# A transformer block's token mixing on one core: another order of projections and convolution taps, and shared softmax steps

## The chip, the core and the metric

The kernel runs on one core of a Trainium2 chip. A core has a matrix engine (TensorE; PE in the profile, with its weight loads as PEld), three engines for everything else (VectorE, DVE; ScalarE, ACT; GpSimd, POOL) and a queue for data transfers (SyncE, SP). Each engine takes its instructions strictly in the order in which the program lists them and waits at an instruction until its inputs are ready and its output's place is free. [...]

The metric is device time in microseconds (us) of one execution. The time before is 1881.29 us, the median of three runs.

## The reference

One layer on 512 tokens of width 2048, all in 32-bit floats. Three mixers share one input projection and one output projection, and a feed-forward part follows:

```python
h = _rms_norm(x, norm1_g[l])
proj = h @ w_in[l]
aq, ak, av, bu, bg, cq, ck, cv = jnp.split(proj, splits, axis=-1)
aq = _rms_norm(aq.reshape(B, S, A_HEADS, HEAD_DIM), a_q_g[l])   # ak, cq, ck likewise
out_a = _dilated_mixture(aq, ak, av).reshape(B, S, A_WIDTH)     # 8 heads x 64
out_b = _conformer_conv(bu, bg, conv_w[l], conv_b[l], conv_ln_g[l], conv_ln_b[l])
out_c, _ = _band_attention(cq, ck, cv, C_WINDOW - 1, sinks=c_sinks[l])
x = x + jnp.concatenate([out_a, out_b, out_c], axis=-1) @ w_out[l]
h2 = _rms_norm(x, norm2_g[l])
x = x + (jax.nn.silu(h2 @ w_gate[l]) * (h2 @ w_up[l])) @ w_down[l]
```

- **A**: 8 heads; three causal patterns of keys (the last 128, every 4th, every 16th), combined by their softmax denominators.
- **B**: 512 channels; `u * sigmoid(gate)`, a causal convolution of each channel over 31 tokens, a layer norm over channels, `silu`.
- **C**: 16 query heads on 2 key heads, the last 128 keys, and a learned sink for each head: the row maximum is `max(scores, sink)` and `exp(sink - maximum)` joins the denominator.

## The kernel before

Tokens lie along the free axis and channels along the 128 partitions, so a tile is 128 channels by 512 tokens. Each 32-bit operand is split into a high and a low part, and a product is three matmuls (`mm3`, lines 311 to 314): high by high, high by low, low by high.

**Stages.** The norm and the first four projection tiles (the A values) come first. Then 26 projection tiles follow one after the other in the order of `PROJ`; a name is mixer, kind and number, so `cq3` holds the queries of C heads 3 and 11, and `bu0` and `bg0` the input and gate of the first convolution tile. While TensorE projects, the other engines work on tiles already projected: the head norms, the two attentions, and the convolution, whose 124 taps (4 tiles of 31) are one VectorE instruction each (`tap`, line 507). Then comes the output projection, in two halves of 8 rows each in the order of `ROWS`, and the feed-forward part, where the change touches nothing.

**Ticks.** The order is written by hand with a clock of ticks (`Ticks`). A step is put down for a number of ticks from now; the program calls `tick()` between matmuls, and what is due then is listed behind the matmuls already listed. A tick is no time but a place in the order of every engine. A projection has 8 ticks with 6 matmuls between two of them, so the 26 projections hold ticks 0 to 207. The first two output tiles share 8 ticks of 6 matmuls (`first_two`); after that a tick stands behind every 12 matmuls, except in the first tile of the second half, where each of its 8 rows (3 matmuls) has one.

**What is due when.**

- `head_scales` (line 561): after a query or key tile is projected, the transpose comes `SQ` = 3 ticks later, then the square, the sum (`total`) and the power -1/2 on GpSimd (`power`, line 586), one tick each.
- `do_k` (line 613) goes on from there: 2 ticks later `widen` copies the scales to a full tile (line 623), then a transpose (`flip`, line 630), `scale`, the copies of each head's 64 rows to the other half (`twin`, two transfers), and after `TD` = 2 ticks the high and low parts (lines 648, 653). `box["k at"]` is the tick before which no head may start on this key.
- `attention` (A) and `grouped_attention` (C) take the first tick that the keys, the queries and the head before allow (`head_at`), and put down each head from there: `scores`, `top` (the maximum and minus its scaled value), `exps` (with the row sums), `norm` (the division), the transposes of the probabilities (`flip`), their high and low parts, the product with the values (`weigh`), and the two halves of its sum. An A head takes 7 ticks, a C head 6; C heads come in pairs that share a key head, one tile of probabilities each.
- `Head` (line 728) holds the small statistics of one head. For C a unit `u` is two of the four 128-token tiles, so `top`, `exps` and `norm` run twice for each head: on VectorE lines 784 and 786 (minus the maximum, with the sink), 803 and 808 (the denominator and its reciprocal), on ScalarE line 798 (the sink's exponential), on GpSimd line 811 (the division).
- `split_mix` (line 986) makes the high and low part of a row of the output projection; the low part of a C row is GpSimd's (line 991), of the others VectorE's. Where a row is not in place when its matmuls come, `split_rows` makes it there.
- The taps start at tick `TAPS_FROM` = 19 and follow every 1.6 ticks, with a pause of 9 ticks from tick 205; the layer norm (`ln_sum` to `ln_out`) follows at fixed distances.

Weights come through SP in the order in which they are used; each is split by ScalarE (line 289) and VectorE (line 290) two units ahead of its use.

Of the kernel before, what the change touches and what calls it, by code (L numbers as in the profile page):

```python
# [9 lines left out]
F32 = mybir.dt.float32  # L10
# [22 lines left out]
TAP_TICKS = 1.6  # L33
TAPS_FROM = 19
# [5 lines left out]
SQ, VD, TD, EV = 3, 4, 2, 1  # L40
# [82 lines left out]
def kernel(ctx: ExitStack, tc: tile.TileContext, xT, wi, wo, wgu, wd, cst_in, outT):  # L123
# [604 lines left out]
    class Head:  # L728


        def __init__(self, kind, box, name, h, number):
# [3 lines left out]
            d = cp.tile([P, 4, NT], F32, name=f"{self.name}d", tag="soft", bufs=6)  # L735
            self.mx, self.nm, self.den, self.rd = (d[:, i] for i in range(4))
            self.banks, self.es = {}, {}

        def start(self, t0):
            _, _, step, s1, sx, s2, *_ = C_TICKS if self.grouped else A_TICKS  # L740
            for u in range(len(self.us)):
# [3 lines left out]
                ticks.after(tu + s1 + sx, self.exps, u)  # L745
                ticks.after(tu + s1 + sx + s2, self.norm, u)
# [16 lines left out]
        def top(self, u):  # L763
# [13 lines left out]
            for i, k0, n, o in reversed(self.us[u]):  # L777
                if self.grouped and i:
# [4 lines left out]
                                               accum_out=mx[:, i:i + 1])  # L783
            nc.vector.scalar_tensor_tensor(nm[:, s], mx[:, s], -1.0, rq[:, s, h], op0=ALU.mult, op1=ALU.mult)
            if self.grouped:
                nc.vector.tensor_scalar(nm[:, s], nm[:, s], nsink[:, self.number:self.number + 1], None, op0=ALU.min)

        def exps(self, u):
# [8 lines left out]
            if self.grouped:  # L797
                nc.scalar.activation(self.mx[:, s], self.nm[:, s], AF.Exp, bias=col(C_SINK + self.number))

        def norm(self, u):  # L800
            e, den, rd, s = self.es[u], self.den, self.rd, self.tiles(u)
            if self.grouped:
                nc.vector.tensor_add(den[:, s], den[:, s], self.mx[:, s])
            else:
                for i, k0, n, o in self.us[u]:
                    nc.vector.scalar_tensor_tensor(e[:, o:o + n], e[:, o:o + n], 1.0, mult_a[:, T - n:],
                                                   op0=ALU.mult, op1=ALU.mult, accum_out=den[:, i:i + 1])
            nc.vector.reciprocal(rd[:, s], den[:, s])
            if self.grouped:
                own = e[:, 2 * u * P:2 * (u + 1) * P].rearrange("p (i k) -> p i k", k=P)  # L810
                nc.gpsimd.tensor_mul(own, own, rd[:, s, None].to_broadcast([P, 2, P]))
                return
# [86 lines left out]
    def grouped_attention(two):  # L899
# [6 lines left out]
        def heads(h):  # L906
# [68 lines left out]
            for t in range(2):  # L975
                ticks.after(t0 + at_flip + t, flip, t)
# [689 lines left out]
```

## Time and profile before

| | |
|---|---|
| median of three runs (1879.92 to 1881.71) | 1881.29 us |
| the profiled execution | 1881.01 us |
| its span, first to last instruction | 1879.0 us |
| TensorE busy | 1868.2 us, 9784 matmuls |
| VectorE busy | 1458.2 us, 2347 instructions |
| ScalarE busy | 1333.2 us, 1886 instructions |
| GpSimd busy | 1219.5 us, 812 instructions |
| mean granted TensorE clock | 0.998 of full |

In a row, `out<-in` names tiles as the program does, and L and a number is a line of the kernel. "a <- b" in a list of waits means that a's engine stood idle until b was done. A matmul's duration in a row is longer than the distance from one to the next, since they overlap. The granted clock is the share of full speed that the chip's throttle gave TensorE. Idle time of an engine matters only if a chain from it reaches the last instruction.

### The profile page before, as it was taken

The numbers are of one execution on the slowest core, as the hardware profiler recorded it, in microseconds if no ns is written. First come the engines' busy times: TensorE is split into PE (matmuls) and PEld (weight loads), VectorE is DVE, ScalarE is ACT, GpSimd is POOL, SyncE is SP. The second block draws the span as 40 slices with busy tenths as digits, with TensorE's granted clock in tenths as the row PEclk, the third lists the DMA queues.
The fourth block names the chain that finished last, engine by engine and source line by source line (L and its number), as shares of the span: only waits on it lengthen the run. The fifth ranks groups of instructions, "written<-read, shape, count | busy, mean of one in ns | idle before, by whom it ended". The sixth has DMA issues, their size and how long they took to land.

```text
span 1879.0 us, 28424 instructions
## 1 busy us (share of the span) xinstructions
PE 1868.2 (99%) x9784; PEld 1605.4 (85%) x9784; DVE 1458.2 (78%) x2347; ACT 1333.2 (71%) x1886; POOL 1219.5 (65%) x812
## 2 busy tenths in 40 slices
PE   9999999999999999999999999999999999999999
PEld 7888878888888888888888888888888888888888
DVE  7578988997679777777777777777777677778887
ACT  6345545553556888888878888788887887777675
POOL 5014433462155878787877878788787867766786
PEclk9999999999999999999999999999999999999999
DMA  7333332434342354443544435344455475578984
GB/s 271 122 110 108 93 96 85 126 100 145 107 146 88 120 175 145 157 168 130 182 138 163 163 133 183 134 164 161 142 178 192 152 239 184 197 251 285 308 243 124
DMA packets 157984, 301.07 MB, mean 160 GB/s; under 512 B 29968, under 2 KB 69008, under 8 KB 157840
## 3 DMA queue, kind: packets, MB, share of 16 engines
q1 hardware_dynamic: 157696, 299.25, 48.4%
q8 instruction: 77, 1.26, 0.3%
q14 instruction: 67, 0.55, 0.1%
q10 hardware_dynamic: 144, 0.01, 0.0%
HBM read 241.27 MB, written 50.33 MB: 155 GB/s over the span
## 4 chain that ended last, share of the span: by engine, by line
PE 92%; DVE 5%; ACT 1%; issue 1%; POOL 1%; DMA 0%; DVEq 0%; POOLq 0%; ACTq 0%
PE out L1255 51%; PE out L1397 16%; PE o L313 3%; PE o L314 3%; PE o L312 3%; DVE wl L290 1%; PE cq L312 1%; PE cq L314 1%; PE cq L313 1%; DVE y L514 1%; PE in L313 1%; PE in L312 1%; PE in L314 1%; PE ak L314 1%; PE ak L312 1%
## 5 line engine op out<-in xcount | busy, mean ns | idle before, releaser
L1255 PE MATMUL out<-h,wh 128*128 128x512 f32 x2464 | 588.4, 391 | 0.0
L1255 PEld LDWEIGHTS out<-h,wh 128*128 128x128 f32 x2464 | 452.7, 188 | 87.5
L1255 PEld LDWEIGHTS out<-h,wl 128*128 128x128 f32 x2464 | 316.1, 191 | 12.5 <-DVE wl L295 0.4
L1255 PE MATMUL out<-h,wl 128*128 128x256 f32 x2464 | 320.3, 283 | 0.2 <-DVE wl L295 0.2
L1397 PE MATMUL out<-wh,a 128*128 128x512 f32 x896 | 221.2, 389 | 0.0
L1397 PEld LDWEIGHTS out<-wh,a 128*128 128x128 f32 x896 | 168.2, 188 | 34.9
L289 ACT CAST wh<-w 128x1024 fp32r<-128x1024 f32 (+1 forms) x93 | 96.8, 1042 | 129.3 <-PE o L313 43.2
L290 DVE TENSOR_TENSOR wl<-w,wh 128x1024 fp32r<-128x1024 f32 (+1 forms) x93 | 117.1, 1261 | 44.9 <-ACT wh L289 44.5
L1397 PE MATMUL out<-wl,a 128*128 128x512 f32 x448 | 119.7, 389 | 0.0
L1397 PEld LDWEIGHTS out<-wl,a 128*128 128x128 f32 x448 | 84.1, 188 | 17.4
L514 DVE SCALAR_TENSOR_TENSOR y<-bu,cst,y 128x511 f32<-128x511 f32 (+14 forms) x120 | 94.4, 787 | 0.7
L1255 PE MATMUL out<-a,wh 128*128 128x512 f32 x330 | 80.1, 391 | 0.0
L1255 PEld LDWEIGHTS out<-a,wh 128*128 128x128 f32 x330 | 60.3, 188 | 11.4
L312 PE MATMUL o<-mh_c,wh 128*128 128x512 f32 x128 | 51.2, 400 | 0.0
L313 PE MATMUL o<-ml_c,wh 128*128 128x512 f32 x128 | 50.1, 392 | 0.5 <-POOL ml_c L991 0.5
L314 PE MATMUL o<-mh_c,wl 128*128 128x512 f32 x128 | 50.1, 391 | 0.0
L1442 DVE TENSOR_TENSOR Y<-Y,out 128x512 f32<-128x512 f32 x48 | 30.7, 682 | 19.4 <-PE out L1397 19.3
L1255 PEld LDWEIGHTS out<-a,wl 128*128 128x128 f32 x330 | 43.3, 191 | 2.2
L1255 PE MATMUL out<-a,wl 128*128 128x256 f32 x330 | 44.1, 283 | 0.0
L312 PE MATMUL cq<-hh,wh 128*128 128x512 f32 x96 | 39.3, 410 | 0.0
L430 POOL TENSOR_TENSOR ssum<-ssum,sq 128x512 f32<-128x512 f32 x15 | 26.8, 1785 | 19.1 <-ACT sq L429 18.6
L314 PE MATMUL cq<-hh,wl 128*128 128x512 f32 x96 | 38.3, 399 | 0.0
(3395 smaller groups left out, 5170.7 us busy)
## 6 DMA issues: line engine op xcount, KB each, us to landing
od<-a SPq DMA_DIRECT2D x140, 256.0 KB, 4.7
a<-od SPq DMA_DIRECT2D x140, 256.0 KB, 6.4
w<-in_wi SPq DMA_DIRECT2D x59, 512.0 KB, 3.6
w<-in_wo SPq DMA_DIRECT2D x32, 512.0 KB, 3.5
x<-in_xT SPq DMA_DIRECT2D x16, 256.0 KB, 7.4
xr<-in_xT SPq DMA_DIRECT2D x16, 256.0 KB, 3.7
x2d<-xr SPq DMA_DIRECT2D x16, 256.0 KB, 2.0
yd<-z SPq DMA_DIRECT2D x16, 256.0 KB, 5.3
```

Source lines behind the costliest of these rows:

```text
L289: nc.scalar.copy(hi[:, :n], t[:, :n])
L290: eng.tensor_sub(lo[:, :n], t[:, :n], hi[:, :n].bitcast(F32))
L312: nc.tensor.matmul(out, wh, xh, start=start, stop=False)
L313: nc.tensor.matmul(out, wh, xl, start=False, stop=False)
L314: nc.tensor.matmul(out, wl, xh, start=False, stop=stop)
L430: eng.tensor_add(acc, acc, sq)
L514: nc.vector.scalar_tensor_tensor(yconv[j][:, i:], hconv[j][:, :T - i], c, yconv[j][:, i:], op0=ALU.mult, op1=ALU.add)
L1255: nc.tensor.matmul(out, lhs[:, s], rhs, start=begin, stop=last and low == flip[0] and x is xs[-1], skip_group_check=True)
L1397: nc.tensor.matmul(to[h], x[:, h * P:(h + 1) * P], v[:, j], start=sub == 0 and h not in started, stop=sub == 1 and n in (len(todo) - 1, le ...
L1442: nc.vector.tensor_add(t, t, b)
```

## The change

- **Order of projections.** `bu1` and `bg1` come right behind `bu0` and `bg0`, before any C tile; `bu2` and `bg2` come two tiles earlier. The host lays the weight columns out in the new order.
- **Taps.** The first 47 steps from tap to tap are one tick each, the later ones 1.8 ticks, and the last two tiles' taps are 6 ticks later on top. The layer norm follows the last tap by two ticks.
- **Keys.** `KW` = 4 ticks instead of 2 between the power and `widen`; `k at` grows by `KW`.
- **C heads.** The statistics of the two heads of a pair share one tile. Minus the maximum and the sink are taken once for each head, for all four token tiles, after the second unit's maximum, and the sink's exponential once with the second unit; the first unit's exponentials come one tick later. The denominator and its reciprocal are taken once for both heads together, and GpSimd divides each head's whole tile in one instruction; all of it stands at the tick where the second head's second unit was divided before.
- **Rows.** Another order of the C rows in the output projection (`w_out` is laid out to match), and three of them instead of two are split during the last projection, at ticks 1, 3 and 5 of it.

```diff
-TAP_TICKS = 1.6
-TAPS_FROM = 19
+TAPS_FROM, TAPS_FAST, TAP_TICKS = 19, 47, 1.8
+TAPS_2 = 6
...
-SQ, VD, TD, EV = 3, 4, 2, 1
+SQ, KW, VD, TD, EV = 3, 4, 4, 2, 1
...
-PROJ = ("av0 av1 av2 av3 bu0 bg0 cv ck cq0 cq3 bu1 bg1 cq1 cq5 cq2 "
-        "cq7 bu2 bg2 ak2 cq4 cq6 bu3 bg3 ak0 aq0 ak1 aq1 aq2 ak3 aq3").split()
-ROWS = "c0 c1 c2 c4 c5 c3 c7 c6 a0 a1 b2 b1 b0 b3 a2 a3".split()
+PROJ = ("av0 av1 av2 av3 bu0 bg0 bu1 bg1 cv ck cq0 cq3 cq1 cq5 bu2 "
+        "bg2 cq2 cq7 ak2 cq4 cq6 bu3 bg3 ak0 aq0 ak1 aq1 aq2 ak3 aq3").split()
+ROWS = "c0 c3 c1 c5 c2 c7 c4 c6 a0 a1 b2 b1 b0 b3 a2 a3".split()
...
-            ticks.after(2, widen, r)
+            ticks.after(KW, widen, r)
-        box["k at"] = ticks.now + SQ + TD + 10
+        box["k at"] = ticks.now + SQ + KW + TD + 10
@@ Head.start @@
-                ticks.after(tu + s1 + sx, self.exps, u)
-                ticks.after(tu + s1 + sx + s2, self.norm, u)
+                if not self.grouped:
+                    ticks.after(tu + s1 + sx, self.exps, u)
+                    ticks.after(tu + s1 + sx + s2, self.norm, u)
+                else:
+                    ticks.after(t0 + step + s1 + 1 + u, self.exps, u)
@@ Head.top @@
+            if self.grouped and u == 0:
+                return
+            if self.grouped:
+                s = slice(0, NT)
             nc.vector.scalar_tensor_tensor(nm[:, s], mx[:, s], -1.0, rq[:, s, h], op0=ALU.mult, op1=ALU.mult)
             if self.grouped:
-                nc.vector.tensor_scalar(nm[:, s], nm[:, s], nsink[:, self.number:self.number + 1], None, op0=ALU.min)
+                nc.vector.tensor_scalar(nm, nm, nsink[:, self.number:self.number + 1], None, op0=ALU.min)
@@ Head.exps @@
-            if self.grouped:
-                nc.scalar.activation(self.mx[:, s], self.nm[:, s], AF.Exp, bias=col(C_SINK + self.number))
+            if self.grouped and u == 1:
+                nc.scalar.activation(self.mx, self.nm, AF.Exp, bias=col(C_SINK + self.number))
@@ Head.norm @@
-                nc.vector.tensor_add(den[:, s], den[:, s], self.mx[:, s])
...
-                own = e[:, 2 * u * P:2 * (u + 1) * P].rearrange("p (i k) -> p i k", k=P)
-                nc.gpsimd.tensor_mul(own, own, rd[:, s, None].to_broadcast([P, 2, P]))
@@ grouped_attention, heads @@
+            d = cp.tile([P, 4, 2, NT], F32, name=f"{name}d2", tag="softs", bufs=2)
+            for k, one in enumerate(pair):
+                one.stats(d[:, :, k])
+            def norm():
+                _, top, den, rd = (d[:, i].rearrange("p k i -> p (k i)") for i in range(4))
+                nc.vector.tensor_add(den, den, d[:, 0].rearrange("p k i -> p (k i)"))
+                nc.vector.reciprocal(rd, den)
+                for k, one in enumerate(pair):
+                    own = one.es[0].rearrange("p (i k) -> p i k", k=P)
+                    nc.gpsimd.tensor_mul(own, own, one.rd[:, :, None].to_broadcast([P, NT, P]))
...
+            ticks.after(t0 + step + s1 + sx + s2, norm)
...
-        at_tap = TAPS_FROM + int(n * TAP_TICKS)
-        ticks.after(at_tap + TAP_PAUSE * (at_tap >= PAUSE_FROM), tap, j, i)
-    t_ln = TAPS_FROM + 1 + int(len(taps) * TAP_TICKS) + TAP_PAUSE
+        at_tap = TAPS_FROM + min(n, TAPS_FAST) + int(max(n - TAPS_FAST, 0) * TAP_TICKS) + TAPS_2 * (j >= 2)
+        at_tap += TAP_PAUSE * (at_tap >= PAUSE_FROM)
+        ticks.after(at_tap, tap, j, i)
+    t_ln = at_tap + 2
...
-            for n, row in enumerate(ROWS[:2]):
-                ticks.after(4 + n, split_mix, row)
+            for n, row in enumerate(ROWS[:3]):
+                ticks.after(1 + 2 * n, split_mix, row)
```

More of the change, by code (lines that the diff above doesn't have):

```diff
@@ L734, in __init__, with stats @@
             self.number = number
-            d = cp.tile([P, 4, NT], F32, name=f"{self.name}d", tag="soft", bufs=6)
+            self.banks, self.es = {}, {}
+        def stats(self, d):
             self.mx, self.nm, self.den, self.rd = (d[:, i] for i in range(4))
-            self.banks, self.es = {}, {}
         def start(self, t0):
@@ L838, in head @@
             one = Head("a", box, mi, h, None)
+            one.stats(cp.tile([P, 4, NT], F32, name=f"{mi}{h}d", tag="soft", bufs=2))
             ph, pl = {}, {}
```

10 lines of the change are left out of this document (3 added, 7 removed).

## The prediction

> **What bounds the kernel now.** I read the page's busy shares first, then the list of who waited for whom on TensorE (columns: waiter, releaser, total us, times, longest).
>
> ```profile
> PE 1868.2 (99%) x9784; PEld 1605.4 (85%) x9784; DVE 1458.2 (78%) x2347; ACT 1333.2 (71%) x1886; POOL 1219.5 (65%) x812
> ```
>
> ```profile
> PE ak2t L630 <- ACT ak2wide L623: 3.8, 1, 3.8
> PE idle L410 <- DVE bones L343: 1.4, 1, 1.4
> PE ak1t L630 <- ACT ak1wide L623: 0.8, 1, 0.8
> PE a10s L758 <- DVE ak1l L653: 0.8, 1, 0.8
> PE o L313 <- POOL ml_c L991: 0.5, 2, 0.3
> PE out L1255 <- DVE wl L295: 0.2, 1, 0.2
> ```
>
> TensorE is busy 99% of the span and idle 7.5 us in all. The change adds and removes no matmul, so it can return only these waits, and what they drag behind them. Work taken from VectorE, ScalarE or GpSimd is worth nothing by itself: it counts only where it shortens one of these six lines, or makes a seventh. The longest has a second price, which stands in windows of 2 us (length, busy time of each engine, granted clock, DMA):
>
> ```profile
> 256.00:258.00 2.00, 0.00 (x0) 0.00 (x0) 2.00 (x4) 0.46 (x1) 1.50 (x1) 0.65 0.00 0
> 258.00:260.00 2.00, 1.79 (x7) 1.60 (x8) 0.44 (x3) 1.74 (x7) 0.61 (x1) 0.50 0.73 209
> 260.00:262.00 2.00, 2.00 (x6) 1.62 (x5) 1.94 (x4) 0.00 (x0) 0.00 (x0) 0.50 0.48 127
> 262.00:264.00 2.00, 2.00 (x7) 1.52 (x7) 0.91 (x3) 0.16 (x1) 0.61 (x1) 0.65 0.85 181
> ...
> 354.00:357.00 3.00, 2.21 (x12) 1.60 (x11) 2.94 (x6) 1.37 (x3) 2.27 (x2) 1.00 0.19 22
> ```
>
> After 3.8 us without work TensorE restarts at half clock. Lost work is busy time times the missing share: 1.79 x 0.50 + 2.00 x 0.50 + 2.00 x 0.35 = 2.6 us. So this one wait costs 3.8 + 2.6 = 6.4 us. The last row holds one of the waits of 0.8 us: its clock stays 1.00, so I price those at 0.8 each. The Trainium skill (TensorE: Matmul & The Clock Gate, section Terms) prices throttled time at time x (1 - K/N); the rows hold (0.35 + 0.50 + 0.50 + 0.35) x 2.0 / 0.50 = 6.8 us at half clock, so an estimate by that page is 3.4, and 0.8 more would come back. The trace bears it out only in part, since the clock had fallen 1.6 us before TensorE had work again.
>
> **The change, part by part.** All ticks below are the planner's arithmetic: a projection is 8 ticks of six matmuls, so the projection with place n in the order after the first four ends before tick 8n.
>
> *The key chain (KW).* The chain behind the 3.8 us, in order of time:
>
> ```profile
> 253.30 0.39 PE L314 MATMUL cq<-h,wl 128*128 128x512 f32 x1
> 253.98 0.39 PE L314 MATMUL cq<-h,wl 128*128 128x512 f32 x1
> 254.21 1.69 POOL L933 TENSOR_TENSOR c20bl<-c20pl,mask_c 128x512 fp32r<-128x512 f32 x1 [1.36 <-DVE c20pl L927]
> 255.87 1.63 POOL L586 TENSOR_TENSOR ak2r<-ak2v,nhalf 128x8 f32<-128x8 f32 x1
> 257.54 0.62 ACT L623 COPY ak2wide<-ak2r 128x512 f32<-128x512 f32 x1 [3.49 <-POOL ak2r L586]
> 258.21 1.12 PE L630 MATMUL ak2t<-ident,ak2wide 128*128 128x128 f32 x4 [3.84 <-ACT ak2wide L623]
> ```
>
> The power on GpSimd stands behind a mask product of an earlier head pair; ScalarE and TensorE, in order, block one after the other. ak2 ends at tick 120 in both orders. The transpose moves from tick 129 to 131: two ticks, twelve matmuls of 0.227 us (the first two rows are three matmuls apart, 0.68 us), 2.7 us. Also, in the new order the pair before it starts at ticks 103 and 109 instead of 105 and 111 (pairs now run from 67 without a gap, every 12 ticks), so its mask products are due by tick 124, two ticks ahead of the power at 126, not level with it. Without the 1.69 us product in front the widened row would stand at 258.2 - 1.7 = 256.5; TensorE asked for it at 258.21 - 3.84 = 254.4 and now asks 2.7 later, at 257.1. **Gain 6.4**; at the worst end, with the product still in front, 258.2 - 257.1 = 1.1 us remains, too short for the clock if the 0.8 us row is any guide (gain 5.3). The ak1 transpose gets the same 2.7 us against 0.8: gain 0.8. The a1 heads wait for "k at", which grows by 4 while the key's low part is due only 2 ticks later, so the 0.8 for ak1l goes too: gain 0.8. In all **8.0**. What the wait queues is ScalarE's exponentials; they now run before the widening. The two copies of a key between partition halves are issued two ticks later on SP, behind a weight load at worst; the two ticks added to "k at" cover that, and one tick more lateness would cost a head's score matmul about a tick, 1.4 us.
>
> *Convolution tiles first, 47 taps at one a tick.* Between ticks 19 and 66 there were 30 taps and are 48; the first heads leave that stretch (start 67, not 49). VectorE has the room (busy time is its third number):
>
> ```profile
> 63.00:97.00 34.00, 34.00 (x154) 28.17 (x153) 16.73 (x22) 10.46 (x14) 1.29 (x1) 1.00 0.31 100
> 97.00:131.00 34.00, 34.00 (x164) 28.39 (x163) 27.04 (x50) 15.56 (x30) 6.18 (x4) 1.00 0.45 132
> 201.00:242.00 41.00, 41.00 (x219) 35.05 (x217) 38.75 (x93) 24.22 (x66) 18.46 (x18) 1.00 0.28 90
> ```
>
> The taps of line 514 alone, busy time of VectorE, and its wait at the first tile's first tap:
>
> ```profile
> 76.00:121.00 45.00, 13.29 (x19) 1.00 0.36 111
> ```
>
> ```profile
> DVE y L512 <- POOL bu L505: 2.1, 1, 2.1
> ```
>
> A tap takes 13.29 / 19 = 0.70 us; 18 more are 12.6 us against 24 us free in the first two rows. TensorE gains nothing from it directly. If the cover were gone, heads from tick 67 on would find VectorE up to 12.6 us late. The third row is what the earlier taps relieve: 38.75 of 41 us busy just ahead of the stall. The fourth tile's first tap is now two ticks behind its gate (152, 154); VectorE then waits about as it did for the first tile (2.1 us), with head steps behind it, which have ticks to spare. The layer norm moves up 8 ticks, from 227 to 219; its first matmul is two ticks later in both.
>
> *Small softmax steps.* For C heads, VectorE's busy time in the four groups that shrink, from 120 to 340 us (lines 784, 786, 803, 808 in this order):
>
> ```profile
> 120.00:340.00 220.00, 9.85 (x32) 0.98 0.34 100
> 120.00:340.00 220.00, 7.31 (x32) 0.98 0.34 100
> 120.00:340.00 220.00, 7.35 (x32) 0.98 0.34 100
> 120.00:340.00 220.00, 5.32 (x32) 0.98 0.34 100
> ```
>
> The 128 small VectorE steps become 16 + 16 + 8 + 8 = 48: 9.85 / 2 + 7.31 / 2 + 7.35 / 4 + 5.32 / 4 = 11.7 instead of 29.8, so 18 us less, 2.3 per pair. Beside TensorE this is worth 0, but it keeps the lead that the first part needs. It makes one thing later: GpSimd now scales whole heads, two products of 512 columns after the last score, where two of four smaller products were done before. The exponentials of unit 0 come one tick later and hold a score bank that much longer; no bank wait stands in the list, so 0.
>
> ```profile
> 238.82 0.17 DVE L808 RECIPROCAL c70d<-c70d 128x2 f32<-128x2 f32 x1
> 239.13 0.61 POOL L811 TENSOR_TENSOR c70e<-c70e,c70d 128x256 f32<-128x256 f32 x1 [0.96 <-DVE c70d L808]
> 243.82 0.27 PE L916 MATMUL c20t<-ident,c20e 128*128 128x128 f32 x1
> ...
> 319.10 0.17 DVE L808 RECIPROCAL c61d<-c61d 128x2 f32<-128x2 f32 x1
> 319.41 1.50 POOL L811 TENSOR_TENSOR c61e<-c61e,c61d 128x256 f32<-128x256 f32 x1 [0.36 <-DVE c61d L808]
> 324.64 0.27 PE L916 MATMUL c41t<-ident,c41e 128*128 128x128 f32 x1
> ```
>
> A product of 512 columns on GpSimd (count, then busy us and mean ns):
>
> ```profile
> L505 POOL TENSOR_TENSOR bu<-bu,bg 128x512 f32<-128x512 f32 x3 | 4.1, 1355 | 6.7 <-ACT bg L504 6.7
> ```
>
> From the reciprocal to the transposes there are 4.8 and 5.4 us; two products of 1.36 need 2.7. Cost 0, upper bound under the rivals.
>
> *The A heads start 4 ticks later.* Key readiness puts a0 at 179 (was 175) and the rest follow; the last head goes from 226 to 230, its weighing from tick 244 to 248. Tick 244 is the first of the output projection's second half, where a tick is only three matmuls, and the last of its eight rows is a3. Before:
>
> ```profile
> 508.40 0.40 PE L312 MATMUL o<-mh_a,wh 128*128 128x512 f32 x1
> 509.94 0.62 ACT L990 CAST mh_a<-mix_a 128x512 fp32r<-128x512 f32 x1 [0.76 <-DVE mix_a L884]
> 510.59 0.69 DVE L991 TENSOR_TENSOR ml_a<-mix_a,mh_a 128x512 fp32r<-128x512 f32 x1 [0.69 <-ACT mh_a L990]
> 512.51 0.39 PE L312 MATMUL o<-mh_a,wh 128*128 128x512 f32 x1
> ```
>
> 508.40 is the first matmul behind the weighing. Counted from it, the row's high part is ready after 2.2 us (510.56) and its low part after 2.9 (511.28); TensorE needed them after 4.1 and 4.3. Moved four ticks, only two rows, six matmuls, 1.4 us, are left between. The high part is 0.8 late; the low part then 2.9 - (1.4 + 0.8 + 0.2) = 0.5 more. **Cost 1.3**, once. Lower bound 0, if TensorE is held elsewhere in those ticks; upper 2.6, since the last probabilities pass ScalarE and VectorE in the same short ticks ahead of the weighing (0.62 + 0.69, were none of it covered). I take 1.3, by the rows of this very chain.
>
> *Rows.* Three C rows are split before the output projection instead of two, but the a1 head's products now fall among the splits on GpSimd. The 0.5 us for ml_c stays (0 to 1.2, one split's 1.3 us less its lead).
>
> **Sum.** The profiled execution took 1881.0 (span 1879.0 and 2.0 around it), 0.3 below the median of the three runs. 1881.0 - 8.0 + 1.3 = 1874.3, beside the median **1874.6**.
>
> **Rivals.** *All waits vanish*, ml_c (0.5) and L295 (0.2) with them, and the a3 row is covered: 1881.3 - 8.7 = 1872.6. For it: VectorE is relieved. Against it: the four ticks are in the planner's arithmetic.
>
> *The key does not do what it says*: VectorE and GpSimd are as late as before, 1.1 us stays at ak2 and both 0.8 stay: 1874.6 + 1.1 + 1.6 = 1877.3. Against it: the freed product in front of the power.
>
> *The stall only moves*: a new wait as long as the old one, with its half clock, at the a3 row or where A heads crowd the first output rows: 1874.6 - 1.3 + 6.4 = 1879.7. For it: late heads are squeezed twice. Against it: I find 1.3 to 2.6 there, and the rows of 0.8 keep their clock. The Trainium skill (same page, Part 1) has the clock fall only after an idle window of about 3.4 us; here 3.8 did it and 0.8 did not.
>
> *Slower*: the whole-head products hold the transposes of all eight pairs. A half product takes 0.61 in one row above and 1.50 in the other, 2.5 times; were whole ones stretched so from 1.36, two would need 6.8 against 5.1 between reciprocal and transposes, 1.7 us of waiting in each pair, 13.6 in all: 1874.6 + 13.6 = 1888.2. It makes the kernel slower from 6.7 / 8 = 0.84 us per pair, products above 3.0 us each. Against it: the 1.36 is itself a mean taken beside VectorE's work. The Trainium skill (SBUF — State Buffer, Who interferes with whom) has the later of the two engines block for the other's whole instruction; the 1.50 agrees, and longer products would then hold VectorE longer too, which this price leaves out.
>
> **How the numbers follow.** Forecast 0.55 (own range 1873.3 to 1875.9), all vanish 0.12, key fails 0.10, stall moves 0.14, slower 0.09. Faster by over 0.2% (about what a measurement of this kernel can tell from no change) means below 1877.5: the first three, 0.77; the moved stall is within 0.2%: 0.14; slower 0.09. The range 1871.8 to 1879.8 reaches from a little under the second case to the middle of the moved stall, and leaves out that case's dearer half and the slower one, 0.16.
>
> **What would show it.** The ak2t, ak1t and a10s lines gone from TensorE's waits; a granted clock of 1.00 from 240 to 280 us; a new line for mh_a or ml_a of 0.8 to 2.6 us near 500 us; about 80 VectorE instructions fewer, and none of TensorE's. Waits at the transposes on line 916's product, or any clock below 1.00 after 20 us, would make it wrong.

## The result, and the profile after

| | before | after |
|---|---|---|
| median of 8 runs each on one chip | 1880.89 us (1879.92 to 1881.71) | 1886.03 us (1883.23 to 1886.83) |
| ratio, 95% interval | | 1.0026 (1.0015 to 1.0037) |
| the profiled execution, and its span | 1881.01 us, 1879.0 | 1883.23 us, 1881.5 |

The change costs 5.1 us (1886.03 - 1880.89), where 6.7 to be gained were forecast: the sign is wrong. The profiled execution of after is the fastest of its eight, so its trace shows less than the median loses.

The busy shares after (engine, busy us, share of the span, instructions):

```profile
PE 1867.7 (99%) x9784; PEld 1602.6 (85%) x9784; DVE 1450.3 (77%) x2267; ACT 1326.7 (71%) x1870; POOL 1215.7 (65%) x796
```

VectorE has the 80 instructions fewer that were counted, TensorE has the same matmuls. The list of who waited for whom on TensorE, after:

```profile
PE c00s L759 <- DVE ck L658: 1.7, 1, 1.7
PE c51s L759 <- DMA cq<-cq2lo: 1.7, 1, 1.7
PE a0o L873 <- DVE a0pl L859: 1.5, 2, 1.0
...
PE o L312 <- ACT mh_a L1004: 0.7, 1, 0.7
PE c40t L929 <- POOL c60e L922: 0.7, 1, 0.7
PE a00s L762 <- DVE ak0l L653: 0.6, 1, 0.6
...
PE o L313 <- DVE ml_a L1005: 0.3, 1, 0.3
```

What was forecast is there: ak2t, ak1t and a10s are gone, and the a3 row waits 0.7 + 0.3 = 1.0 us (1.3 forecast). And the clock stays up where it had fallen; a window of after (length, busy times, then the granted clock in the third column from the end):

```profile
240.00:280.00 40.00, 40.00 (x219) 34.32 (x218) 34.71 (x70) 22.37 (x64) 17.11 (x13) 1.00 0.34 98
```

But new lines have come elsewhere: at the first C head (c00s), at a later pair's scores (c51s) and transposes (c40t), at A's first head (a00s, a0o). The C key's own chain is late. TensorE's row says VectorE; ScalarE's list of waits has what stands behind that:

```profile
ACT ckh L648 <- DMA ck<-ck: 6.7, 1, 6.7
```

The transfers after (count, KB each, median us from issue to landing):

```profile
ck<-ck SPq DMA_DIRECT2D x2, 128.0 KB, 4.2
```

The same row of before:

```profile
ck<-ck SPq DMA_DIRECT2D x2, 128.0 KB, 2.3
```

The two copies between partition halves take 4.2 us instead of 2.3. ScalarE, in order, stands 6.7 us at the key's high part (3.6 in changed_c_key_back below, where only the key's chain is put back); VectorE makes the low part after it, and TensorE waits 1.7 us for that.

### The profile page after: what moved, and what is told of

Its sections match the earlier page's. It is cut to its first block, busy times and chain, and to the rows that moved or that the text cites. A ratio compares the mean times of both kernels' runs of the same rounds, so it can differ in the third digit from the quotient of the medians.

```text
span 1881.5 us, 28295 instructions
## 1 busy us (share of the span) xinstructions
PE 1867.7 (99%) x9784; PEld 1602.6 (85%) x9784; DVE 1450.3 (77%) x2267; ACT 1326.7 (71%) x1870; POOL 1215.7 (65%) x796
## 4 chain that ended last, share of the span: by engine, by line
PE 87%; DVE 9%; ACT 2%; issue 1%; DMA 1%; DVEq 0%; SPq 0%; ACTq 0%
PE out L1270 51%; PE out L1412 16%; PE o L313 2%; PE o L312 2%; PE o L314 2%; DVE wl L290 2%; DVE y L514 1%; PE in L313 1%; PE in L314 1%; PE in L312 1%; PE cq L313 1%; PE cq L312 1%; PE cq L314 1%; PE aq L312 1%; PE aq L314 1%
## 5 line engine op out<-in xcount | busy, mean ns | idle before, releaser
L505 POOL TENSOR_TENSOR bu<-bu,bg 128x512 f32<-128x512 f32 x4 | 5.7, 1422 | 54.9 <-ACT bg L504 54.9
```

The lines of the kernel that those rows point to most:

```text
L505: nc.gpsimd.tensor_mul(hconv[j], hconv[j], t)
```

## The experiments

Each kernel below was timed in turn with the kernel before on one chip; ratios are against that, with their 95% intervals. The kernel before had medians of 1879.86 to 1880.20 us in these comparisons, and 1880.89 beside the change; so where two kernels were timed in different comparisons, I compare what each lost or gained against the kernel before beside it. An interval is some 0.1% to either side, about 2 us: a difference of 1 or 2 us between two kernels is not clear of it.

### One part alone, and all but one

*Softmax steps alone.* The kernel before with the changes to `Head` and to `norm` in `grouped_attention`:

```diff
-                ticks.after(tu + s1 + sx, self.exps, u)
+                    ticks.after(t0 + step + s1 + 1 + u, self.exps, u)
...
+            ticks.after(t0 + step + s1 + sx + s2, norm)
```

> The kernel before with the small softmax steps shared, and nothing else. Theory 1 (holding the first unit's score bank until both units' maxima are done makes TensorE wait for a bank, and the whole-head products hold the transposes): a wait of 1 to 2 us at a C score matmul and one or two of about 0.7 at transposes come in, while ak2t shrinks a little because GpSimd and VectorE are relieved: 1879 to 1884, not under 1878. Theory 2 (18 us less on VectorE is lead that shortens the waits, and the loss is all the taps'): ak2t at most 2 us with a full clock, no new wait: 1873 to 1877.

1880.81 us (1879.26 to 1882.77), ratio 1.0003 (0.9993 to 1.0012): no difference.

*Order and taps alone.* `PROJ`, the tap constants and the ticks of `tap` and `ln_sum`:

```diff
-TAP_TICKS = 1.6
-TAPS_FROM = 19
+TAPS_FROM, TAPS_FAST, TAP_TICKS = 19, 47, 1.8
+TAPS_2 = 6
```

> The kernel before with the new order of projections and the new tap calendar, and nothing else. Theory 1 (part of the loss): the first C score waits 1.7 us or more for the key's low part, ak2t stays between 2 and 4 us: 1881 to 1885. Theory 2 (the crowded stretch from tick 19 to 66 and C heads without a gap are the whole loss): 1886 or more, with several waits on VectorE from 140 us on. If the moved order relieves the ak2 chain by itself, as the prediction had it, ak2t is gone and the time is under 1878.

1880.75 us (1879.28 to 1882.57), ratio 1.0001 (0.9991 to 1.0010): no difference, though the trace is another one. TensorE's largest waits there:

```profile
PE lnm L535 <- DVE part L533: 2.7, 1, 2.7
PE ak1t L630 <- ACT ak1wide L623: 2.0, 1, 2.0
```

The 3.8 us at ak2t have gone with the new order and taps, without any later widening, and others have taken their place: the one at lnm is new, ak1t has grown from 0.8, two at a1t make 1.7.

*Rows alone.*

```diff
-ROWS = "c0 c1 c2 c4 c5 c3 c7 c6 a0 a1 b2 b1 b0 b3 a2 a3".split()
+ROWS = "c0 c3 c1 c5 c2 c7 c4 c6 a0 a1 b2 b1 b0 b3 a2 a3".split()
...
-            for n, row in enumerate(ROWS[:2]):
-                ticks.after(4 + n, split_mix, row)
+            for n, row in enumerate(ROWS[:3]):
+                ticks.after(1 + 2 * n, split_mix, row)
```

> The kernel before with the new order of C rows and three of them split during the last projection, and nothing else. Both theories: only the two ml_c waits (0.5 us) can change, so 1880.5 to 1881.5, the same as before within what can be measured.

1881.29 us (1880.93 to 1882.49), ratio 1.0003 (0.9993 to 1.0012): no difference.

*The keys' ticks alone.*

```diff
-            ticks.after(2, widen, r)
+            ticks.after(KW, widen, r)
-        box["k at"] = ticks.now + SQ + TD + 10
+        box["k at"] = ticks.now + SQ + KW + TD + 10
```

> The kernel before with the key's widening 4 ticks behind the power instead of 2, and nothing else. Before is 1880.9. Theory 1 (the loss comes from new waits of TensorE that the softmax steps and the moved taps each make; the key's later widening is worth what it was priced at): ak2t falls from 3.8 us to at most 1.1, the clock stays full, ak1t and a10s go, the a3 row waits 1.3 to 1.5: 1874 to 1876. Theory 2 (the key's delay only shifts the A heads and the stall with them): 1879 to 1883, with a new wait above 3 us or waits of A heads (a0o, a2o, mh_a) that sum to 6 us.

1886.08 us (1881.84 to 1887.36), ratio 1.0028 (1.0018 to 1.0038): slower by as much as the whole change, and outside both expected ranges. c00s waits 2.3 us, a0o 2.1 and a C row's low part (ml_c) 2.2; ak2t, ak1t and a10s wait no more.

*All of the change but the keys' ticks*, the same two lines put back in the changed kernel:

> The changed kernel with the key's widening back at 2 ticks behind the power and the old start of heads; the other parts as changed. Theory 1 (KW alone is the loss, and the rest together is worth the relief of the ak2 chain): c00s no longer waits, ak2t is at most 2 us, 1875 to 1880. Theory 2 (the parts' losses add up on any calendar, and KW only happens to show them): 1882 to 1885, with the wait of c51s for its bank (1.7) and of c40t for the whole-head product (0.7) still there and new A head waits.

1878.55 us (1878.13 to 1880.57), ratio 0.9993 (0.9984 to 1.0003). So the loss lies in those two lines, and what is left of the change gains at most a little. TensorE still waits 2.0 us there at ak1t and 2.0 at lnm. The lines hold four things: two ticks on the C key's chain, four on its heads, and the same for the A keys.

### The lines of the keys, one thing at a time

*Only ak2's widening later*, the one key whose wait is 3.8 us; no head moves:

```diff
-            ticks.after(2, widen, r)
+            ticks.after(4 if name == "ak2" else 2, widen, r)
```

> The kernel before with the widening of ak2 alone 2 ticks later; no head starts later, since a2 starts at tick 205 anyway. If the 3.8 us and its half clock are really worth 6.4, as the prediction priced them, and only the other keys did the harm: ak2t at most 1.1, clock full from 20 us on, 1873.5 to 1876. If TensorE's time is made up again elsewhere (VectorE's backlog only surfaces at the next wait): 1878 to 1881, with ak1t or an A head waiting 2 us or more.

**1876.56 us** (1875.57 to 1878.14), ratio 0.9983 (0.9974 to 0.9993): faster than both kernels. Two ticks do what they were meant to, and the wait is gone without a successor of its size; TensorE's largest, behind the 1.4 us of the start:

```profile
PE ak1t L630 <- ACT ak1wide L623: 0.8, 1, 0.8
...
PE c40o L946 <- POOL c40bl L933: 0.7, 1, 0.7
```

The same line put into the kernel without the keys' ticks:

> The changed kernel with the later widening for ak2 alone, and no ticks added between any key and its heads. If the loss lies in the C key and the places of the A heads, the waits at c00s, c51s, c40t and the a3 row are gone, ak2t stays gone, and the time is that of the changed kernel without the key's ticks or a little below: 1876 to 1878.5 us, 8 to 10 under the changed kernel. If the loss lies in the softmax steps, the taps or the rows, it stays above 1882 us.

1878.94 us (1878.08 to 1879.92), ratio 0.9994 (0.9985 to 1.0004): no gain over 1878.55, and a little above the expected 1876 to 1878.5. In the new order ak2t no longer waits, so there is nothing left for these ticks to remove.

*All heads four ticks later, no chain moved:*

```diff
-        box["k at"] = ticks.now + SQ + TD + 10
+        box["k at"] = ticks.now + SQ + TD + 14
```

> The kernel before with the heads' earliest tick 4 later (k at) and the widening itself where it was. Theory 1a (the harm of KW is that the A heads come 4 ticks later, into other steps): a0o waits for a0pl about 2 us, the ml_c and mh_a waits of the changed key are there, ak2t stays 3.8: 1885 to 1890. Theory 1b (the harm is that the copies of the key fall behind weight loads in the transfer queue and ScalarE waits for them): no wait at c00s; only the a3 row's 1.4 is added and a10s goes: 1880.5 to 1882.

1887.08 us (1886.35 to 1887.87), ratio 1.0040 (1.0025 to 1.0055). The places of the heads alone, with no key later, cost 7.2 us.

*The C key alone, chain and heads:*

```diff
+            ticks.after(4 if gi else 2, widen, r)
...
+        box["k at"] = ticks.now + SQ + TD + (14 if gi else 10)
```

> The kernel before with the later widening and the later heads for the C key alone. Theory 1b: its two copies are issued behind three weight loads instead of ahead of them, ScalarE's first split of the key waits for them 4 us or more longer, and the first C score waits about 2.3 us as in the run with KW for all keys; ak2t stays: 1882.5 to 1885. Theory 1a: the C key has no part in it: 1879.5 to 1881.5.

1883.32 us (1882.48 to 1888.04), ratio 1.0020 (1.0011 to 1.0029).

TensorE's new wait in it (ak2t's has grown too, from 3.8 to 4.4):

```profile
PE c00s L755 <- DVE ck L658: 2.6, 1, 2.6
```

Its transfers:

```profile
w<-in_wi SPq DMA_DIRECT2D x4, 512.0 KB, 4.9
...
ck<-ck SPq DMA_DIRECT2D x2, 128.0 KB, 5.8
```

In SP's order of issue (start, us, transfer) the copies now stand behind three weight loads that they had led before:

```profile
111.92 1.75 SPq L277 DMA_DIRECT2D w<-in_wi  x3
114.64 1.29 SPq L642 DMA_DIRECT2D ck<-ck  x2
```

*The same, with the two copies issued by ScalarE*, past SP's queue:

```diff
+                (nc.scalar if gi else nc.sync).dma_start(both[h][HALF[1 - h]], both[h][HALF[h]])
```

> The C key alone two ticks later, and its heads four, as in kw_ck_only (1883.3 us), but the key's two half copies are issued by ScalarE, not by SP. Theory A, the copies land late because they stand behind three weight loads in SP's queue: landing returns from 5.8 to some 2.3 us, ScalarE no longer waits 8.2 us for the copied halves, TensorE's wait of 2.6 us at c00s goes, and the time is 1880 +- 1. Theory B, the copies are late because the DMA engines are full of weights, whatever the queue: landing stays above 4 us, the wait at c00s stays above 1.5 us, 1883 +- 1.5. Theory C, the copies are not what costs: the wait goes, but the time stays at 1883, since the C heads four ticks later cost it.

1882.95 us (1882.56 to 1885.92), ratio 1.0019 (1.0009 to 1.0028). The first theory, a place in SP's queue, falls. Its transfers:

```profile
ck<-ck ACTq DMA_DIRECT2D x2, 128.0 KB, 5.3
```

TensorE's wait:

```profile
PE c00s L755 <- DVE ck L658: 2.0, 1, 2.0
```

A window of 2 us while they are under way (last columns: clock, busy share of the transfer engines, GB/s):

```profile
116.00:118.00 2.00, 2.00 (x10) 1.68 (x9) 1.61 (x4) 0.00 (x0) 1.66 (x1) 1.00 1.00 272
```

From another queue the copies still take 5.3 us, and in this window the transfer engines are full. What the slow landings have in common is that loads of 512 KB were issued first. The Trainium skill (DMA: Bandwidth & Descriptors, section Issuing engines are not separate DMA queues) says that transfers of all issuing engines end up on the same 16 engines and that a second issuer saves only issue time; 5.3 against 5.8 us agrees.

### Why the A heads cost more than their last row

*Only the A heads four ticks later*, and *two*:

```diff
+        box["k at"] = ticks.now + SQ + TD + (10 if gi else 14)
```

> The kernel before, with 4 ticks more between the key and the heads of the A rows alone; no widening is moved and the C heads stay. Theory A, it is the A heads' new places that cost the 7.2 us of kat_only: waits of about 2 us at a0o, about 1 each at ak3t and at the first A head's transposes, the a3 row's 1.0, and 1885 to 1888 us. Theory B, my prediction's price (1.3 us for the a3 row, less the 0.8 for ak1l): 1880 to 1881 us, and what kat_only lost lies with the C heads.

> The same with 2 ticks in place of 4. Theory A, a gradual cost, each tick of lateness squeezing the last A head against the short ticks of the output rows: no a3 wait yet or a small one, and about half of what 4 ticks cost. Theory B, it is a matter of which steps meet on VectorE and GpSimd at the new ticks: the waits are others than with 4 ticks, and the time can be anything from 1878 to 1888 us, not half.

Four ticks: 1887.36 us (1885.82 to 1887.75), ratio 1.0037 (1.0024 to 1.0050). That is `kat_only`'s time, where the C heads were moved too: in the kernel before, four ticks on the C heads cost nothing that shows. Two ticks: 1880.57 us (1880.13 to 1883.87), ratio 1.0006 (0.9996 to 1.0016), not half of it, and not to be told from nothing. With four, TensorE's waits:

```profile
PE a0o L871 <- DVE a0pl L857: 2.1, 2, 1.7
...
PE a0t L846 <- POOL a00e L814: 1.1, 1, 1.1
PE o L312 <- ACT mh_a L990: 0.7, 1, 0.7
```

Windows of it, with VectorE's busy time as the third:

```profile
364.00:368.00 4.00, 2.90 (x15) 2.23 (x14) 3.90 (x12) 3.76 (x8) 2.90 (x2) 1.00 0.59 199
...
372.00:376.00 4.00, 4.00 (x23) 3.44 (x22) 2.50 (x6) 1.43 (x3) 1.79 (x2) 1.00 0.60 180
376.00:380.00 4.00, 2.29 (x11) 1.53 (x9) 2.75 (x8) 0.60 (x1) 0.49 (x1) 0.99 0.38 82
380.00:384.00 4.00, 3.58 (x12) 3.06 (x13) 3.83 (x12) 1.27 (x3) 1.38 (x1) 0.58 0.33 106
```

a0t's wait ends at 366.7 us, in a window where VectorE is busy 3.90 of 4 us; GpSimd's division, which it waits for, stood 5.67 us until VectorE's reciprocal was done. That is crowding. The a0o waits end at 378.0 and 380.4, and in the 8 us up to 380 VectorE is not full (2.50 and 2.75 of 4): it stands idle itself ahead of the second of a0's low parts, by the profile until TensorE's own first product:

```profile
377.21 0.69 DVE L857 TENSOR_TENSOR a0pl<-a0t,a0ph 128x512 fp32r<-128x512 f32 x1 [2.68 <-PE a0o L870]
```

The third low part comes 2.7 us later, behind a tap of 0.73 and other steps. After these waits TensorE runs 3.58 us at 0.58: another 3.58 x 0.42 = 1.5 us. To tell VectorE's load from the heads' places, 17 taps of that stretch were **left out**, so these two kernels do not compute the last convolution tile in full:

```diff
-        ticks.after(at_tap + TAP_PAUSE * (at_tap >= PAUSE_FROM), tap, j, i)
+        if not 178 <= at_tap < 205:
+            ticks.after(at_tap + TAP_PAUSE * (at_tap >= PAUSE_FROM), tap, j, i)
```

> a_heads_4_later (1887.4 us) with the 17 convolution taps of ticks 178 to 204 left out, so the convolution's last tile is not the reference's; 17 taps of about 0.7 us take 12 us from VectorE in the stretch where the A heads run. Theory A, the A heads cost so much because VectorE, 98% busy there, reaches a0's low part late: the 2.1 us at a0o and the half clock behind it go, most of the 1.7 us at a0t and ak3t too, the a3 row's 0.9 stays, and the time is 1880.5 to 1882 us. Theory B, the heads' own steps or GpSimd are late at their new ticks: the waits stay and it takes 1885 to 1888 us.

> The kernel before with the same 17 taps left out: what the missing taps are worth by themselves. Both theories: at most the 1.5 us of ak1t and a10s, so 1878 to 1880 us, and ak2t with its 3.8 us stays. Were it far below, a_heads_4_fewer_taps would have to be read against this run and not against the kernel before.

With the A heads late: 1880.32 us (1880.00 to 1882.26), ratio 1.0000 (0.9991 to 1.0010). Without: 1878.16 us (1876.83 to 1879.59), ratio 0.9990 (0.9981 to 0.9999). So four ticks cost 7.5 us with the taps (1887.36 - 1879.86) and 2.2 us without them. Waits of the first:

```profile
PE a0o L871 <- DVE a0pl L857: 1.0, 1, 1.0
...
PE o L312 <- ACT mh_a L990: 0.7, 1, 0.7
```

The a3 row's 0.7 us does not depend on the taps. 5.3 of the 7.5 us go with them: a0t's wait, half of a0o's and the fall of the clock behind it. How the taps bring the a0o waits about is not shown: without them VectorE stands idle at the same low part even longer, 4.6 us, and there the profile names the landing of a copy of aq2.

### Inside the changed kernel

In the kernel before the parts add up: 3.4 for the C key and 7.5 for the A heads, less the 3.3 gained at ak2, make 7.6, and the keys' ticks together cost 6.1, the same within the intervals. The other parts of the change could alter each of them, so each was undone in the changed kernel.

*The C key and its heads as before; A as changed:*

```diff
-            ticks.after(KW, widen, r)
+            ticks.after(2 if gi else KW, widen, r)
-        box["k at"] = ticks.now + SQ + KW + TD + 10
+        box["k at"] = ticks.now + SQ + TD + (10 if gi else 14)
```

> The changed kernel with the C key and its heads at the ticks of before; the A keys stay 2 ticks later and their heads 4. Theory A, the two costs add: the waits at c00s, c51s and c40t go, those at a0o and the a3 row stay, and the time is 3 to 5 us under the changed kernel, 1881 to 1883 us. Theory B, the A heads alone are the loss: 1885 to 1887 us. Theory C, the C key alone is the loss, since the softmax steps free VectorE for the A heads: 1878 to 1880 us.

*The A keys and their heads as before; C as changed*, with `KW if gi else 2` and `14 if gi else 10`:

> The changed kernel with the A keys and their heads at the ticks of before; the C key stays 2 ticks later and its heads 4. Theory A: the wait at c00s of 1.7 to 2.6 us and c51s's 1.7 stay, the waits at a0o, a2o and the a3 row go, and the time is 1881 to 1884 us. Theory B (A heads alone): 1878 to 1880 us. Theory C (C key alone): 1885 to 1887 us.

*Only the C key's chain as before; its heads stay four ticks later*, the first of the two lines alone:

> The changed kernel with the C key's widening, and so its two copies, at the ticks of before; its heads stay four ticks later, as in the changed kernel. Theory A, the late copies are the loss: landing is 2.3 us again, the wait at c00s goes, and the time is near that of changed_c_back, 1876 to 1878.5 us. Theory B, the heads' places are the loss (all pairs of C heads four ticks later, with a score bank held one tick longer): c00s goes, but c51s's 1.7 us and c40t's 0.9 stay, and it takes 1882 to 1886 us.

| kernel | us (lowest to highest) | against the kernel before beside it | ratio, 95% interval |
|---|---|---|---|
| changed_c_back | **1876.76** (1876.29 to 1877.73) | -3.4 | 0.9982 (0.9972 to 0.9991) |
| changed_c_key_back | 1881.98 (1881.61 to 1882.77) | +2.0 | 1.0011 (1.0001 to 1.0020) |
| the change | 1886.03 (1883.23 to 1886.83) | +5.1 | 1.0026 (1.0015 to 1.0037) |
| changed_a_back | 1889.47 (1888.56 to 1891.55) | +9.3 | 1.0050 (1.0035 to 1.0065) |

The C key is the whole loss: without its ticks the change beats the kernel before by 3.4 us, more than any of the three theories allowed. Its later heads cost 2.0 + 3.4 = 5.4 us, clear of the intervals. Its later chain costs 5.1 - 2.0 = 3.1; the two intervals just overlap, so this size is the less certain. TensorE's waits with only the heads late:

```profile
...
PE c51s L759 <- DMA cq<-cq2lo: 1.2, 1, 1.2
...
PE c40t L929 <- POOL c60e L922: 0.7, 1, 0.7
PE a00s L762 <- DVE ak0l L653: 0.6, 1, 0.6
PE c21t L929 <- DVE mix_c L977: 0.4, 1, 0.4
```

and with the C key wholly as before (the a3 row's two lines are those of the change):

```profile
PE a0o L873 <- DVE a0pl L859: 1.5, 2, 1.0
...
PE a2o L873 <- DVE a2pl L859: 0.3, 1, 0.3
PE lnm L535 <- DVE a21e L811: 0.3, 1, 0.3
...
PE a10s L762 <- DVE ak1l L653: 0.2, 1, 0.2
```

The clock at its two a0o waits, in windows of 4 us:

```profile
368.00:372.00 4.00, 2.52 (x12) 1.84 (x11) 3.10 (x8) 0.65 (x2) 1.49 (x1) 0.94 0.46 98
372.00:376.00 4.00, 4.00 (x15) 3.24 (x15) 3.83 (x11) 1.81 (x4) 1.22 (x2) 0.63 0.43 131
```

c51s, c40t, c21t and a00s go with the C heads' four ticks, c00s with the key's two. SP's issues say how little the latter takes. With the C key as before:

```profile
136.37 1.19 SPq L642 DMA_DIRECT2D ck<-ck  x2
137.64 0.54 SPq L277 DMA_DIRECT2D w<-in_wi  x1
```

In the change:

```profile
135.39 0.47 SPq L277 DMA_DIRECT2D w<-in_wi  x1
136.73 1.21 SPq L642 DMA_DIRECT2D ck<-ck  x2
```

The copies are issued 0.36 us later, but behind one weight load instead of ahead of it, and land after 4.2 us instead of 2.3. The A keys' two ticks and their heads' four, taken together, are even worth having here. Undone as well (all of the change but the keys' ticks, -1.3 us) they leave the kernel 2.1 us slower than changed_c_back. Undone alone (changed_a_back, above all three expected ranges) they cost 4.1 more than the change. The intervals overlap a little in both cases, but the traces say the same: without them ak1t waits 2.0 and lnm 2.0 in the first kernel; ak1t 2.9, ak0t 2.1, a00s 2.0 and lnm 1.9 in the second, with the clock near 0.6 in two windows of 4 us. In changed_c_back ak1t does not wait and lnm waits 0.3. So what the later widening removes in the new order is ak1t's wait, not ak2t's.

*The change with the softmax steps of before:*

```diff
-                    ticks.after(t0 + step + s1 + 1 + u, self.exps, u)
+                ticks.after(tu + s1 + sx, self.exps, u)
...
-            ticks.after(t0 + step + s1 + sx + s2, norm)
```

> The changed kernel with the softmax steps of before, so that the exponentials of a C head's first half run a tick earlier and its score bank is freed a tick earlier; the key's ticks, order, taps and rows are those of the change. If the longer held bank is behind c51s, that wait of 1.7 us goes, c40t's wait behind a whole-head product too, and the time is 2 to 4 us under the changed kernel, 1882 to 1884 us, with c00s's wait still there. If c51s waits for something else, it stays and the time is 1885 to 1887 us, or more, since VectorE has 18 us more to do.

1890.34 us (1890.08 to 1891.22), ratio 1.0052 (1.0037 to 1.0067): 10.4 us above the kernel before, 5.2 more than the change and not less. At c51s the wait is down and has another releaser, but many waits stand where the change has none: seven at L946, the sum of weighted values, 3.3 us together, and one at another pair's scores (c71s), for which the profile names no releaser ("issue"):

```profile
PE c71s L755 <- issue: 1.7, 1, 1.7
...
PE c51s L755 <- ACT c11e L796: 0.4, 1, 0.4
```

So the steps cost 1.3 us at c51s and earn more elsewhere. The waits at L946 are for GpSimd's masked products and VectorE's low parts: with the C heads late, these two engines need the work taken off them.

## Why the prediction was wrong

In short: the forecast wait at ak2t goes, and the sign is lost at the C key, at two steps of the sum. Its heads, four ticks later, had no term (5.4 us measured), and its two copies were called covered (3.1).

**Key chain: right in mechanism, its 6.4 us too large.** ak2t's wait goes, and no wait of its size follows. In the profiled executions it is worth what was worked out: the span falls from 1879.0 to 1873.6 us with that line alone, 5.4, which is 6.4 less the new 0.7 at c40o and other small ones. By medians it is 1879.88 - 1876.56 = 3.3 us. The term was sized on one execution, and the clock's part of it, 2.6 us, is not the same in each. Up to 264 us a_heads_2_later runs the same program as the kernel before, and its ak2t waits 3.8 us too; yet less of it runs at half clock (window of the kernel before, then the same of a_heads_2_later; clock in the third column from the end):

```profile
256.00:264.00 8.00, 5.79 (x17) 4.74 (x18) 5.29 (x11) 2.36 (x8) 2.73 (x3) 0.57 0.51 129
256.00:264.00 8.00, 6.45 (x30) 5.61 (x31) 5.17 (x11) 3.81 (x10) 2.07 (x3) 0.79 0.61 149
```

In the second the clock's part is 6.45 x 0.21 = 1.4 us, not 2.6. The profiled execution of before has a mean clock of 0.998; of the kernel's 120 executions beside the experiments 32 have that, 82 have 0.999 and 6 have 1.000. At these lengths of half clock (6.9 and 3.4 us of 1879) the mean would be 0.998 and 0.999, so most seem to pay the smaller part or none. The order was half of the reasoning for this term, and with the new order and taps the wait goes without any later widening (taps alone); there it is ak1t, with 2.0 us, that needs it.

**The two copies: one step that failed.** 'Behind a weight load at worst; the two ticks added to "k at" cover that' named the very load, and nothing of it was priced from a row. Behind one load landing goes from 2.3 to 4.2 us (behind three, in the kernel before, to 5.8), ScalarE stands 6.7 us at the key instead of 3.6, and VectorE's low part comes after it. The two ticks did not cover that. The text's own price for a late key, 1.4 us, was near what c00s shows (1.7); the later chain costs 3.1.

**The C heads four ticks later: the larger step, a term that is missing.** I priced the A heads' four ticks and not the C heads', of which I said only where they start. In the changed kernel they cost 5.4 us, though in the kernel before they cost nothing that shows (`kat_only` against the A heads alone). In the profiled executions the spans differ by 1880.1 - 1875.4 = 4.7, of which 1.2 + 0.7 + 0.6 + 0.4 = 2.9 are the four waits shown; the rest is not traced to a wait:

- c51s, 1.2, is by all signs the bank priced at 0 ("no bank wait stands in the list"; a bank is the accumulator that holds a head's scores until its exponentials have read them). In after's trace c11's exponentials on its first bank are held up by c11's minus maximum, which both units now share and which comes after the second unit's maximum, and TensorE starts when those on the first bank end (start, us, engine, tile):

```profile
218.58 0.46 ACT L804 ACTIVATE c11e<-c11s,c11d,cq1r 128x128 f32<-128x128 f32 x1 [3.58 <-DVE c11d L794]
...
219.03 0.45 ACT L804 ACTIVATE c11e<-c11s,c11d,cq1r 128x128 f32<-128x128 f32 x1
219.50 0.35 PE L759 MATMUL c51s<-ck,cq 128*128 128x256 f32 x1 [1.71 <-DMA cq<-cq2lo]
```

The releaser in brackets is the copy of a query tile; 219.03 + 0.45 = 219.48 and 219.50 speak for the exponential, and without the shared steps the profile itself names c11e. Softmax steps alone show no such wait, and `kat_only` with its late heads neither; it takes both.

- c40t, 0.7, is the "slower" rival's mechanism, at one pair of eight: the whole-head products start late because the product of a convolution gate is in front of them on GpSimd, which stood 5.97 us until ScalarE had the gate ready:

```profile
302.62 1.29 POOL L505 TENSOR_TENSOR bu<-bu,bg 128x512 f32<-128x512 f32 x1 [5.97 <-ACT bg L504]
...
304.92 1.03 POOL L922 TENSOR_TENSOR c60e<-c60e,c40d 128x512 f32<-128x512 f32 x1
306.01 0.33 PE L929 MATMUL c40t<-ident,c60e 128*128 128x128 f32 x1 [0.67 <-POOL c60e L922]
```

Not from stretched products, as that rival had it: the 1.03 of the second product (1.10 the first) is below the 1.36 it set out from.

- a00s, 0.6, and c21t, 0.4, come with the same four ticks; their causes were not followed.

**The A heads: the row was right, the place was not looked at.** "Cost 1.3, once" was measured as 1.0 at mh_a and ml_a. But moved heads meet other work: in the kernel before their four ticks cost 7.5 us, 5.3 of it only where the 17 taps stand among them. In the changed kernel a0o waits 1.5 us, and the clock then costs 2.52 x 0.06 + 4.00 x 0.37 = 1.6 more. The sum has both at nothing.

**Without the C key the same arithmetic holds.** For changed_c_back, worked out afterwards from its own list, it reads: ak2t 6.4, ak1t 0.8, a10s 0.6 and ml_c 0.5 gone, 8.3; a0o 1.5 and its clock 1.6, the a3 row 1.0, a2o and lnm 0.3 each come, 4.7; 1881.0 - 8.3 + 4.7 = 1877.4 against 1877.23 profiled. So beside the C key the forecast of 1874.3 lacked a0o and its clock above all.

**Order, taps, rows, softmax at nothing: right alone** (1.0001, 1.0003, 1.0003), for order and taps by luck: there ak2t's wait goes, and waits at lnm, ak1t and a1t with a fall of the clock of their own (0.95 and 0.62 in the two windows of 4 us from 348 us) come in for about as much. "It keeps the lead" was right too, and undersized: in the changed kernel the softmax steps are worth 5.2 us.

**The rivals.** Their shape was right in "the stall only moves", but its place was not among them; none started from the C key.

**What stays open.** After's profiled span exceeds that of changed_c_key_back by 1.4 us, the medians against the kernel before by 3.1. What the slower executions of after lose beside c00s's 1.7 us isn't in a trace. The C heads' ticks were not put back alone, with the chain left late, so their 5.4 us and the chain's 3.1 hold in the one order in which they were undone.

## What to carry to other kernels

When a wait is one instruction's, move that instruction alone: two ticks for one key gained 3.3 us, two ticks for every key and four for every head lost about 6. For each step that is moved, list what it is moved past in the queues and on the transfer engines, and who is next on each engine it can hold up; a "covered" is a claim with two numbers, the lateness and the slack. Removing work beside the bound shows nothing by itself, yet it can decide whether another edit pays: test edits together and with each one left out.

## What the runs showed of the hardware

- **The clock falls after short waits too, and not after each.** I priced only waits of about 3.8 us with it. In changed_c_back two waits at a0o, 1.5 us together and the longer one 1.0, put TensorE at half clock: the rows above hold (0.06 + 0.37) x 4.00 / 0.50 = 3.4 us of it. A wait of 2.0 us at ak1t was followed by 0.62 in taps alone and left the clock at 1.00 in all but the keys' ticks. A wait of 2.6 us at c00s in the kernel without the softmax steps left it alone too (two windows of that kernel; TensorE lacks 2.01 and 0.58 us of work in them, and the clock is 1.00):

```profile
144.00:148.00 4.00, 1.99 (x11) 1.43 (x9) 2.75 (x4) 3.57 (x7) 0.00 (x0) 1.00 0.10 23
148.00:152.00 4.00, 3.42 (x17) 2.91 (x18) 3.96 (x8) 0.27 (x1) 0.00 (x0) 1.00 0.41 149
```

The Trainium skill (TensorE: Matmul & The Clock Gate, Part 1) describes a free-running window of 3413 ns, with half clock after an idle one. The 3.4 us agrees, and so does a dependence on where a wait falls; that the idle time must fill a window does not, where the longer wait was 1.0 us.

- **The clock's price differs between executions of one program.** After the same 3.8 us at ak2t the windows above hold 0.43 x 8.00 / 0.50 = 6.9 us of half clock in one execution and 0.21 x 8.00 / 0.50 = 3.4 in another, two such stretches or one. Of the 120 executions of the kernel before, the 32 whose mean granted clock was 0.998 average 1881.2 us, the 82 with 0.999 1880.0, the 6 with 1.000 1878.7: a step of about 1.2 us for 0.001 of mean clock. A price of a few us read from one profile is uncertain by about that.
- **A small transfer lands later behind large ones already issued:** two copies of 128 KB land after 2.3 us ahead of the weights, 4.2 behind one load of 512 KB, 5.8 behind three, 5.3 behind three from another engine's queue.
